# Loading five per-layer vectors as one row and spreading them with a product of ones

## The chip, the core and the metric

The kernel runs on one core of a Trainium2 chip. A core has five engines with queues of their own: TensorE (PE; its weight loads are listed as PEld), VectorE (DVE), ScalarE (ACT), GpSimd (POOL) and SyncE (SP), and sixteen DMA engines that all queues share. DMAs are issued here from SP, ACT and POOL. The metric is the device time of one execution in microseconds, less is better. The times of before are the median of 3 runs, 846.11 us (844.33 to 847.06).

## The reference

A trunk of two layers over 256 tokens of width 1024. Each layer normalises the stream, projects it once into the inputs of three token mixers (a Mamba-2 scan, sliding-window attention with sinks, forgetting attention), gates each branch, projects it back, merges the branches by sigmoid gates, projects once more and adds the residual.

```python
for layer in range(DEPTH):
    h = rms_norm(x, norm_w[layer])
    proj = jnp.einsum('bsd,de->bse', h, w_in[layer])
    ... = jnp.split(proj, split_at, axis=-1)
    y_a = mamba2_branch(a_xbc, a_z, a_dt, conv_w[layer], conv_b[layer], dt_bias[layer],
                        a_log[layer], d_skip[layer], ssm_norm_w[layer])
    y_b = sliding_window_branch(b_q, b_k, b_v, b_z, sinks[layer], cos, sin)
    y_c = forgetting_attention_branch(c_q, c_k, c_v, c_f, c_z, f_bias[layer])
    ...
```

Five of the parameters are vectors of 16 numbers per layer, one number per head. They enter as follows.

```python
dt = jax.nn.softplus(dt_raw + dt_bias)             # step sizes
a = -jnp.exp(a_log)                                # decay rates
y = y + d_skip[:, :, None] * xh                    # skip factors, one per head of 64 channels
sink = jnp.broadcast_to(sinks, ...)                # one more logit in the softmax
log_f = jax.nn.log_sigmoid(f_logit + f_bias)       # forget gates
```

## The kernel before

**Precision and weights.** Every float32 product of the projections is made of three faster passes: an operand is split into a high and a low part, and high x high, low x high and high x low are accumulated. The weights come in parts of 128 partitions x up to 1024 numbers. Each part is loaded by SP into one of six `raw` buffers (`load_part`, L335), split by ACT into `hi` (L257) and by DVE into `lo` (L258), each with six buffers, and then used by PE (`mm`, L97). A raw buffer is free again when its split is done; a hi and lo buffer when PE has used the part.

**Order.** PE's order is written out: the list `ops` holds the blocks of the projections one after the other, and a small planner (`launch`, `pump`) puts the pieces of the mixers (transposes, attention, scan) between the matmuls, by its own clock of PE time. A DMA or operation under `pin` keeps its place in program order; the other engines' orders are chosen when the program is built.

**The start of the first layer.** The first two blocks, the keys and values of the windowed attention, run on the stream before its normalisation; their results are scaled by the row scales `y.rn`. Then `layer_consts` issues the loads of the layer's constants on POOL's queue, and the query blocks and the block of step sizes (`cols(C_DT, 272)`: 16 step-size logits and 256 queries) follow. After that `normalize` is launched: ACT makes a diagonal of the row scales (L1166), PE multiplies it with ones, DVE scales the stream by the product (L1176), and ACT and DVE split it again into the high and low parts that all later blocks use. This stands beside the first block of the forgetting attention's values (`cv(0, 352)`, two halves of 24 matmuls each).

**The constants.** `layer_consts` loads the convolution's weights, its bias and a norm weight into `vr`, 88 rows, which `layer_vec` transposes on PE and copies into `y.vec`. The four vectors dt_bias, f_bias, sinks and a_log are each loaded to all 128 partitions into `y.hb`. The skip factors go to `y.dsk`, where partitions 0 to 63 hold those of the even heads and 64 to 127 those of the odd heads: two loads to 64 partitions, each taking every second number of the row. `logits` adds the parts of `y.hb` to the step-size and forget logits on DVE (L624, L626); `layer_vec` makes `y.nsink` and `y.nega` from it. In the second layer the loads are issued on ACT's queue, late in the first layer, where the norm weight of the second layer is loaded too. `layer_vec` is called just before the first gate block (`zs(C_ZB, 1)`) in both layers.

Of the kernel before, what the change touches and what calls it, by code (L numbers as in the profile page):

```python
# [13 lines left out]
AF = mybir.ActivationFunctionType  # L14
ALU = mybir.AluOpType

P = 128
S = 256
D = 1024
NK = D // P  # L20
# [24 lines left out]
def hybrid_trunk(  # L45
# [5 lines left out]
    nc = tc.nc  # L51
# [11 lines left out]
    def T(tag, shape, dtype=F32, bufs=None):  # L63
        count[0] += 1
        return sb.tile(shape, dtype, tag=tag, name=f"{tag}_{count[0]}",
                       bufs=bufs if bufs is not None else BUFS.get(tag, 1))
# [11 lines left out]
    act = nc.scalar.activation  # L78
# [172 lines left out]
    def pin(f):  # L251
        return lambda *a, **k: tc.keep_in_program_order(f(*a, **k))  # L252
# [141 lines left out]
    for l in range(L):  # L394
        y = Layer()
# [4 lines left out]
    def layer_consts(y, queue):  # L400
        l = y.l
        pdma = pin(queue.dma_start)
        vr = T("vr", [88, P])
        pdma(vr[0:64, :], conv_w[l].rearrange("j (u p) -> (j u) p", p=P))
        pdma(vr[64:80, :], conv_b[l:l + 1, :].rearrange("o (u p) -> (o u) p", p=P))
        pdma(vr[80:88, :], ssm_norm_w[l:l + 1, :].rearrange("o (u p) -> (o u) p", p=P))
        if l:
            y.nwb = T("nwb", [P, D])
            pdma(y.nwb, norm_w[l:l + 1, :].to_broadcast([P, D]))
            pin(nc.gpsimd.tensor_scalar)(y.nwb, y.nwb, -0.5, None, op0=ALU.mult)  # L410
        y.hb = T("hb", [P, 64], bufs=2)
        for i, v in enumerate((dt_bias, f_bias, sinks, a_log)):
            pdma(y.hb[:, 16 * i:16 * i + 16], v[l:l + 1, :].to_broadcast([P, 16]))
        y.dsk = T("dsk", [P, NK], bufs=2)
        for half in range(2):
            src = d_skip[l:l + 1, :].rearrange("o (j two) -> two o j", two=2)[half]
            pdma(y.dsk[64 * half:64 * half + 64, :], src.to_broadcast([64, NK]))
        y.vr = vr

    def layer_vec(y):  # L420
        p = pmx()
        transpose(p[:, 0:88], y.vr, ident[:88, :88])
        y.vec = T("vec", [P, 88], bufs=2)
        act(y.vec[:, 0:80], p[:, 0:80], AF.Copy, scale=0.5)
        act(y.vec[:, 80:88], p[:, 80:88], AF.Copy, scale=-0.5)
        y.nsink = T("nsink", [P, 16], bufs=2)
        pin(ts)(y.nsink, y.hb[:, 32:48], -1.0, None, op0=ALU.mult)
        y.nega = T("nega", [P, 16], bufs=2)
        pin(act)(y.nega, y.hb[:, 48:64], AF.Exp)
        pin(ts)(y.nega, y.nega, -1.0, None, op0=ALU.mult)  # L430


    def chan(y, w, c):
# [71 lines left out]
    def u_bq(y, c0, t):  # L505

        def f(w):
            p = tok(y.hTh, y.hTl, w, t, turn=w.n == 512)
            if w.n == 272:
                logits(y, t, 0, p[:, 0:16])  # L510
                p = p[:, 16:272]
            for i in range(w.n // 256):
                if t == 0:
                    y.qT[c0 + i] = T("qt", [P, 2, S])
                with tc.high_priority():
                    a, b = rope(y, p[:, i, :] if w.n == 512 else p, t)
                    gtt(a, a, b, op=ALU.add)
                launch(1, rest(c0 + i, a.rearrange("p h d -> p (h d)")), D_Q if y.rn is None else 2.2 * D_Q)
            pump()

        def rest(c, q):
            qT = y.qT[c]
            pt = pmx()
            for j in range(2):
                transpose(pt[:, j * P:(j + 1) * P], q[:, j * P:(j + 1) * P], ident)
            act(qT[:, :, t * P:(t + 1) * P], pt[:, 0:256].rearrange("p (h s) -> p h s", h=2), AF.Copy)
            if t == 1:
                launch(1, swa_quad(y, c, qT), D_QK)
            yield 0.0
        return f  # L530
# [527 lines left out]
    def op(i, *fs):  # L1058
        for f in fs:
            ops.append((i, f))  # L1060

    for y in layers:
        l = y.l
        w = w_in[l]
        y.rn = None
        y.gate, y.qT, y.ckT, y.sz, y.yh, y.yl, y.sq, y.h, y.ss, y.var, y.zdone, y.cqdone = {}, {}, {}, {}, {}, {}, [], {}, {}, {}, set(), {}
        y.u = y.cv = None

        def cols(c0, n=256):
            return sub([(0, w[:, c0:c0 + n])], n)  # L1070

        def cv(c, n):
            op(cols(C_CV + c, n), u_cv(y, c, 0), u_cv(y, c, 1))

        def z1(c0, br, b):
            op(cols(c0 + 256 * b), u_z(y, br, 2 * b, 0), u_z(y, br, 2 * b + 1, P))

        def zs(c0, br):
            for b in range(4):
                z1(c0, br, b)  # L1080

        def gates_proj(br):
            def g(b):
                c = 512 * b
                op(cols(C_G + D * br + c, 512), u_gate(y, br, c, 0), u_gate(y, br, c, 1))

            def p(b):
                c = 512 * b
                if b == 0 and br != 0 and (br, l) != (1, 0):
                    op(None, lambda y=y: split_late(y, br))  # L1090
                i = sub([(0, w_proj[l, br, :, c:c + 512])], 512)
                if b == 0 and br == 0:
                    op(i, u_proj2(y, br))
                else:
                    op(i, u_proj(y, br, c, 0), u_proj(y, br, c, 1))
            seq = [(g, 0), (p, 0), (g, 1), (p, 1)]
            if br == 0:
                seq = [(lambda b: z1(C_ZA, 0, b), b) for b in range(4)] + seq
            return [lambda f=f, b=b: f(b) for f, b in seq]

        if l == 0:
            k, v = cols(C_BK), cols(C_BV)
            op(k, u_bkv(y, 0, 0, {16: lambda: second_rows(0), 20: lambda: second_rows(1)}, lambda: first_end()))
            op(k, u_bkv(y, 0, 1, {}))
            op(v, u_bkv(y, 256, 0), u_bkv(y, 256, 1))
            op(None, lambda: layer_consts(y0, nc.gpsimd))
            for c, n in ((1, 512), (3, 256)):
                op(cols(C_BQ + 256 * c, n), u_bq(y, c, 0), u_bq(y, c, 1))
            op(cols(C_DT, 272), u_bq(y, 0, 0), u_bq(y, 0, 1))
            op(None, lambda: launch(9, normalize(y0), 0.0))  # L1110
            cv(0, 352)
            op(None, lambda: normalized(y0))
        else:
            kv, q3 = cols(C_BK, 512), cols(C_BQ + 768)
            op(None, lambda: drain(5))
            op(kv, u_bkv(y, 0, 0))
            op(q3, u_bq(y, 3, 0))
            op(None, lambda: drain(6))
            op(kv, u_bkv(y, 0, 1))
            op(q3, u_bq(y, 3, 1))  # L1120
            op(cols(C_DT, 272), u_bq(y, 0, 0), u_bq(y, 0, 1))
            op(cols(C_BQ + 256, 512), u_bq(y, 1, 0), u_bq(y, 1, 1))
        op(None, lambda y=y: layer_vec(y))
        zs(C_ZB, 1)
        heavy = [(C_B + 256 * b, 8 + 2 * b) for b in range(4)] + [(C_XS + 256 * b, 2 * b) for b in range(4)]
        gp = gates_proj(1)

        if l == 0:
            lights = {1: [lambda: cv(696, 344)], 3: [lambda: cv(352, 344)], 5: [gp.pop(0)], 6: [lambda: op(None, lambda y=y: split_late(y, 1))], 7: [gp.pop(0)]}
        else:  # L1130
            lights = {0: [lambda: cv(696, 344)], 2: [lambda: cv(0, 352)], 3: [lambda: cv(352, 344)],
                      4: [gp.pop(0)], 6: [gp.pop(0)]}
        for i, (c0, u) in enumerate(heavy):
            op(cols(c0), u_conv(y, u, 0), u_conv(y, u + 1, P))
            for light in lights.get(i, ()):
                light()
        for f in gp:
            f()

        for b, zb in enumerate(((), (0,), (1,), (2, 3))):  # L1140
            op(cols(C_CK + 256 * b), u_ck(y, 2 * b, 0), u_ck(y, 2 * b + 1, P))
            op(cols(C_CQ + 256 * b), u_cq(y, 2 * b, 0), u_cq(y, 2 * b + 1, P))
            for z in zb:
                z1(C_ZC, 2, z)
        for f in gates_proj(0):
            f()
        op(None, load_final if l + 1 == L else lambda: layer_consts(layers[1], nc.scalar))
        for f in gates_proj(2):
            f()
        o = [sub([(0, w_out[l, :, c:c + n])], n) for c, n in ((0, 256), (256, 512), (768, 256))]  # L1150
        pieces_out[l] = o[0]
        op(o[0], u_out2(y, 0))
        for t in range(2):
            for i, c in ((1, 256), (2, 768)):
                op(o[i], u_out(y, c, t, i))
# [163 lines left out]
```

## Time and profile before

| | before |
|---|---|
| median of 3 runs | 846.11 us (844.33 to 847.06) |
| profiled execution, time | 846.84 us |
| profiled execution, span from the first to the last instruction | 844.9 us |
| mean granted clock of TensorE | 0.996 |
| PE busy, matmuls | 830.3 us (98%), 6063 |
| DVE busy | 649.7 us (77%) |
| ACT busy | 509.4 us (60%) |
| POOL busy | 105.4 us (12%) |
| moved by DMA | 157.91 MB, mean 187 GB/s |

In the rows of the profile, `out<-in` names the tiles that an instruction writes and reads, L97 is a line of the kernel, and `[3.06 <-ACT L L1166]` says that the engine stood for 3.06 us before the instruction and that line 1166 on ACT ended the wait. A row of the windows gives, for a stretch of the span, its length and the busy time of PE, PEld, DVE, ACT and POOL with their instructions in brackets; then the granted clock, the mean busy share of the DMA engines and GB/s. A DMA row ends with the time from issue to landing. POOL prepares its own DMAs, so they show as rows of POOL; those of SP and ACT stand under SPq and ACTq.

### The profile page before, as it was taken

What the parts mean: (1) busy time and instruction counts of PE and PEld (TensorE: products, weight loads), DVE (VectorE), ACT (ScalarE), POOL (GpSimd) and SP (SyncE); (2) the same over time, 40 slices, a digit from 0 to 9 for tenths busy, and PEclk for the clock granted to TensorE, in tenths of its full rate; (3) what the DMA queues carried; (4) which work ended last, traced back from release to release, by engine and by line L of the source; (5) the groups of instructions that cost most, each with busy time, mean ns of one, the idle gap of its engine ahead of it and who ended that gap; (6) DMA issues with size and microseconds to landing.
All of it is one profiled execution on the core that took longest, in us unless ns stands there. A gap on an engine that the chain in (4) does not pass through costs nothing. (4 is left out here: it accounts for less than half of the span.)

```text
span 844.9 us, 16259 instructions
## 1 busy us (share of the span) xinstructions
PE 830.3 (98%) x6063; PEld 767.9 (91%) x6063; DVE 649.7 (77%) x1425; ACT 509.4 (60%) x1020; POOL 105.4 (12%) x137
## 2 busy tenths in 40 slices
PE   8989999999999999999999999999999999999996
PEld 7989999988999998888989999999899999988896
DVE  6877898998776669656677889889978567785665
ACT  7367777755666667435455676876557667654442
POOL 3810000100140010210013000100003110121000
PEclk9999999999999999999999999999999999999999
DMA  9876456657565545748567535766765554576632
GB/s 305 175 184 184 118 176 206 228 177 233 157 191 177 179 149 178 237 144 297 196 206 221 159 112 161 231 204 203 224 188 176 175 176 150 163 236 212 212 100 74
DMA packets 124495, 157.91 MB, mean 187 GB/s; under 512 B 7321, under 2 KB 91473, under 8 KB 124417
## 3 DMA queue, kind: packets, MB, share of 16 engines
q1 hardware_dynamic: 108816, 140.53, 53.1%
q10 hardware_dynamic: 15312, 16.28, 6.1%
q0 software_dynamic: 288, 0.08, 1.1%
q8 instruction: 47, 0.77, 0.4%
q14 instruction: 32, 0.25, 0.1%
HBM read 154.70 MB, written 2.16 MB: 186 GB/s over the span
## 5 line engine op out<-in xcount | busy, mean ns | idle before, releaser
L258 DVE TENSOR_TENSOR lo<-raw,hi 128x1024 fp32r<-128x1024 f32 (+3 forms) x262 | 309.1, 1194 | 98.1 <-ACT hi L257 86.4
L97 PE MATMUL mm<-hi,L 128*128 128x512 f32 (+4 forms) x1424 | 378.2, 353 | 1.0 <-ACT L L1216 0.5
L257 ACT ACTIVATE hi<-raw 128x1024 fp32r<-128x1024 f32 (+3 forms) x262 | 263.6, 1022 | 97.3 <-PE mm L97 78.7
L97 PE MATMUL mm<-L,hi 128*128 128x256 f32 x1792 | 318.2, 278 | 0.0
L97 PEld LDWEIGHTS mm<-L,hi 128*128 128x128 f32 x1792 | 277.8, 192 | 7.4 <-issue 3.9
L97 PEld LDWEIGHTS mm<-hi,L 128*128 128x128 f32 x1424 | 252.1, 190 | 27.6 <-issue 2.1
L97 PE MATMUL mm<-lo,L 128*128 128x512 f32 (+4 forms) x712 | 247.7, 349 | 0.0
L97 PE MATMUL mm<-L,lo 128*128 128x256 f32 x896 | 246.4, 275 | 0.0
L97 PEld LDWEIGHTS mm<-L,lo 128*128 128x128 f32 x896 | 171.9, 192 | 0.1
L97 PEld LDWEIGHTS mm<-lo,L 128*128 128x128 f32 x712 | 134.8, 190 | 12.4
L872 POOL TENSOR_SCALAR_AFFINE_SELECT bias<-bias 128x128 f32<-128x128 f32 x64 | 36.4, 604 | 413.3 <-DMA bias<-cumd 286.5
L565 ACT ACTIVATE pp<-pp,nm 128x128 f32<-128x128 f32 (+1 forms) x128 | 56.6, 443 | 14.2 <-DVE nm L559 11.8
L694 DVE SCALAR_TENSOR_TENSOR L<-L,vec,L 128x255 f32<-128x255 f32 (+2 forms) x96 | 46.0, 479 | 2.2 <-ACT L L691 1.2
L697 ACT ACTIVATE L<-L 128x256 f32<-128x256 f32 x32 | 13.3, 417 | 42.0 <-DVE L L694 42.0
L896 ACT ACTIVATE L<-L 128x512 f32<-128x512 f32 x24 | 15.1, 630 | 32.6 <-DVE L L895 32.4
L97 PE MATMUL mx<-L,L 128*64 128x128 f32 (+1 forms) x384 | 34.5, 314 | 0.0
L577 DVE TENSOR_SCALAR pp<-pp,rsum 128x128 f32<-128x128 f32 (+1 forms) x128 | 32.1, 314 | 0.3
L778 ACT ACTIVATE L<-mm 128x256 f32<-128x256 f32 x48 | 18.1, 378 | 20.9 <-PE mm L97 20.9
L97 PEld LDWEIGHTS mx<-L,L 128*64 128x64 f32 x384 | 22.9, 136 | 8.3 <-issue 0.9
L594 ACT ACTIVATE L<-mx 128x512 f32<-128x512 f32 x48 | 26.8, 596 | 1.2 <-PE mx L101 1.0
L101 PE MATMUL mx<-ident,pp 128*128 128x128 f32 x192 | 26.3, 273 | 0.0
L565 ACT ACTIVATION_READ_ACCUMULATOR pp<-pp,nm 128x1 f32 x128 | 23.9, 187 | 0.0
(185 smaller groups left out, 718.9 us busy)
## 6 DMA issues: line engine op xcount, KB each, us to landing
raw<-in_w_in_dram SPq DMA_DIRECT2D x179, 512.0 KB, 4.5
raw<-in_w_proj_dram SPq DMA_DIRECT2D x48, 512.0 KB, 5.1
raw<-in_w_out_dram SPq DMA_DIRECT2D x16, 512.0 KB, 5.1
raw<-in_w_in_dram SPq DMA_DIRECT2D x16, 344.0 KB, 3.3
L<-cumd ACTq DMA_DIRECT2D x8, 512.0 KB, 4.9
bias<-cumd ACTq DMA_DIRECT2D x16, 256.0 KB, 3.6
L<-in_gate_bias_dram ACTq DMA_DIRECT2D x12, 256.0 KB, 4.7
raw<-in_w_in_dram SPq DMA_DIRECT2D x8, 352.0 KB, 3.5
```

What stands on the lines that cost most here:

```text
L97: nc.tensor.matmul(o, a, b, **kw)
L101: nc.tensor.transpose(o, a, i)
L257: keep(act)(hi, src, AF.Copy)
L258: keep(tt)(lo, src, hi.bitcast(F32), op=ALU.subtract)
L565: act(pp[:, i, sl], pp[:, i, sl], AF.Exp, scale=-1.0, bias=nm[:, e:e + 1], accum_out=sums[:, e:e + 1])
L577: ts(pp[:, i, sl], pp[:, i, sl], rs[:, 2 * i + b:2 * i + b + 1], 0.5, op0=ALU.mult, op1=ALU.mult)
L594: act(pT, pt, AF.Copy)
L694: stt(a[:, s:S], x_[:, 0:S - s], y.vec[:, 16 * j + u:16 * j + u + 1], a[:, s:S], op0=ALU.mult, op1=ALU.add)
L697: act(th, a, AF.Tanh)
L778: act(halves(th), p, AF.Tanh, scale=0.5)
L872: nc.gpsimd.affine_select(out=bias[:, i, dst], in_=bias[:, i, src], compare_op=ALU.is_ge, fill=NEG, base=0, pattern=[[-1, P]], channel_mul ...
L896: act(g, g, AF.Tanh, scale=0.5)
```

## The change

The five vectors are loaded into one row `y.hr` of one partition (five loads of 16 numbers). `layer_vec` puts the row on all partitions by a product with a row of ones on PE, into the same PSUM bank as the transpose of `vr`, and ACT copies the result into `y.hb`, now 80 columns wide. The skip factors are arranged from it by two copies on POOL, and `y.nsink` and `y.nega` are made on POOL instead of DVE. Since `y.hb` now comes from `layer_vec`, its call moves ahead of the block of step sizes in both layers.

```diff
-        y.hb = T("hb", [P, 64], bufs=2)
-        for i, v in enumerate((dt_bias, f_bias, sinks, a_log)):
-            pdma(y.hb[:, 16 * i:16 * i + 16], v[l:l + 1, :].to_broadcast([P, 16]))
-        y.dsk = T("dsk", [P, NK], bufs=2)
-        for half in range(2):
-            src = d_skip[l:l + 1, :].rearrange("o (j two) -> two o j", two=2)[half]
-            pdma(y.dsk[64 * half:64 * half + 64, :], src.to_broadcast([64, NK]))
+
+        y.hr = T("hr", [1, 80])
+        for i, v in enumerate((dt_bias, f_bias, sinks, a_log, d_skip)):
+            pdma(y.hr[:, 16 * i:16 * i + 16], v[l:l + 1, :])
         y.vr = vr

     def layer_vec(y):
         p = pmx()
         transpose(p[:, 0:88], y.vr, ident[:88, :88])
         y.vec = T("vec", [P, 88], bufs=2)
-        act(y.vec[:, 0:80], p[:, 0:80], AF.Copy, scale=0.5)
-        act(y.vec[:, 80:88], p[:, 80:88], AF.Copy, scale=-0.5)
-        y.nsink = T("nsink", [P, 16], bufs=2)
-        pin(ts)(y.nsink, y.hb[:, 32:48], -1.0, None, op0=ALU.mult)
+        mm(p[:, 96:176], ones[0:1, :], y.hr, start=True, stop=True)
+        y.hb = T("hb", [P, 80], bufs=2)
+        pin(act)(y.hb, p[:, 96:176], AF.Copy)
+        pin(act)(y.vec[:, 0:80], p[:, 0:80], AF.Copy, scale=0.5)
+        pin(act)(y.vec[:, 80:88], p[:, 80:88], AF.Copy, scale=-0.5)
         y.nega = T("nega", [P, 16], bufs=2)
         pin(act)(y.nega, y.hb[:, 48:64], AF.Exp)
-        pin(ts)(y.nega, y.nega, -1.0, None, op0=ALU.mult)
+        gts = nc.gpsimd.tensor_scalar
+        y.nsink = T("nsink", [P, 16], bufs=2)
+        gts(y.nsink, y.hb[:, 32:48], -1.0, None, op0=ALU.mult)
+        gts(y.nega, y.nega, -1.0, None, op0=ALU.mult)
+        y.dsk = T("dsk", [P, NK], bufs=2)
+        for i in range(2):
+            r = slice(64 * i, 64 * i + 64)
+            nc.gpsimd.tensor_copy(y.dsk[r, :], y.hb[r, 64:80].rearrange("p (j i) -> p i j", i=2)[:, i, :])
...
             for c, n in ((1, 512), (3, 256)):
                 op(cols(C_BQ + 256 * c, n), u_bq(y, c, 0), u_bq(y, c, 1))
+            op(None, lambda y=y: layer_vec(y))
             op(cols(C_DT, 272), u_bq(y, 0, 0), u_bq(y, 0, 1))
...
             op(kv, u_bkv(y, 0, 1))
             op(q3, u_bq(y, 3, 1))
+            op(None, lambda y=y: layer_vec(y))
             op(cols(C_DT, 272), u_bq(y, 0, 0), u_bq(y, 0, 1))
             op(cols(C_BQ + 256, 512), u_bq(y, 1, 0), u_bq(y, 1, 1))
-        op(None, lambda y=y: layer_vec(y))
         zs(C_ZB, 1)
```

## The prediction

> **What bounds the kernel now.** I read the page first (busy times, queues), then the waits of PE, then the timeline around the one long wait, then the windows and the DMA issues of that stretch.
>
> ```profile
> PE 830.3 (98%) x6063; PEld 767.9 (91%) x6063; DVE 649.7 (77%) x1425; ACT 509.4 (60%) x1020; POOL 105.4 (12%) x137
> q0 software_dynamic: 288, 0.08, 1.1%
> ```
>
> PE is busy for 830.3 of 844.9 us, so an edit is worth what it does to PE's queue: work added, waits removed, clock. The second row is the queue of the DMAs that POOL issues: 0.08 MB cost 1.1% of sixteen engines' span, which is 0.011 x 844.9 = 9.3 us on every engine. All POOL DMAs are the loads of the first layer's constants, in one stretch.
>
> ```profile
> PE mx L97 <- ACT L L1166: 3.1, 1, 3.1
> PE mx L101 <- POOL ident masks.py:199: 1.5, 1, 1.5
> ```
>
> The longest wait of PE is one of 3.1 us; the next is at the start. It stands here in the timeline:
>
> ```profile
> 47.85 0.46 PE L97 MATMUL mm<-hi,L 128*128 128x352 f32 x2
> ...
> 48.30 0.46 PE L97 MATMUL mm<-hi,L 128*128 128x352 f32 x2
> ...
> 48.75 0.38 PE L101 MATMUL mx<-ident,L 128*128 128x128 f32 x2
> 50.79 1.06 ACT L257 ACTIVATE hi<-raw 128x1024 fp32r<-128x1024 f32 x1 [5.67 <-DMA raw<-in_w_in_dram]
> 51.75 0.68 ACT L1166 ACTIVATE L<-ident,rs 128x128 f32<-128x128 f32 x2
> ...
> 52.19 1.09 PE L97 MATMUL mx<-L,ones 128*128 128x128 f32 x4 [3.06 <-ACT L L1166]
> ```
>
> Read it backwards. PE waits for the diagonal of row scales (`normalize`); ACT made it only at 51.75, because a weight split stood ahead of it in ACT's order, and that split waited 5.67 us for its weights. The weights were late because the DMA engines were full and moved nothing:
>
> ```profile
> 34.00:38.00 4.00, 4.00 (x35) 4.00 (x35) 1.83 (x5) 0.79 (x1) 3.98 (x7) 1.00 0.95 171
> 38.00:42.00 4.00, 4.00 (x35) 4.00 (x34) 3.31 (x7) 1.09 (x3) 1.59 (x2) 1.00 1.07 38
> 42.00:48.00 6.00, 6.00 (x47) 5.99 (x46) 3.79 (x9) 2.22 (x4) 2.31 (x2) 1.00 0.67 5
> 48.00:52.00 4.00, 1.13 (x9) 0.88 (x7) 0.12 (x1) 1.21 (x2) 0.00 (x0) 1.00 0.91 310
> 52.00:56.00 4.00, 3.81 (x15) 3.81 (x16) 3.88 (x7) 3.49 (x9) 0.00 (x0) 0.57 1.10 351
> ```
>
> The last three columns are granted clock, DMA share and GB/s. From 38 to 48 us the engines show shares of 1.07 and 0.67 at 38 and 5 GB/s. In the last row the clock is 0.57: after its wait PE runs at about half speed for some 4 us.
>
> ```profile
> 31.90 0.37 SPq L335 DMA_DIRECT2D raw<-in_w_in_dram  x1
> 40.83 4.50 SPq L335 DMA_DIRECT2D raw<-in_w_in_dram  x1
> DMA to landing us min/median/max: 3.0/4.4/17.6
> vr<-in_conv_w_dram POOLq DMA_DIRECT2D x1, 32.0 KB, 2.2
> vr<-in_ssm_norm_w_dram POOLq DMA_DIRECT2D x1, 4.0 KB, 3.5
> hb<-in_sinks_dram POOLq DMA_DIRECT2D x1, 8.0 KB, 7.6
> dsk<-in_d_skip_dram POOLq DMA_DIRECT2D x2, 2.0 KB, 14.1
> ```
>
> The weight load that ACT waited for is the one issued at 31.90 (six raw buffers, so its turn comes with the split six parts earlier). The third row is for weight loads between 20 and 70 us: median 4.4, longest 17.6. One issue took 4.50 us instead of 0.37. The two d_skip loads, 2 KB each, take 14.1 us: they are 512 single numbers each, written with a stride over 64 partitions. They are what runs while everything else stands.
>
> **The change part by part.**
>
> (a) The scattered skip-factor loads and the four 128-partition loads go; five loads of one row of 64 bytes come. With them goes the blockage of 38 to 48 us. The load of 31.90 then lands at 31.90 + 4.4 = 36.3, an estimate from the median. What is late next?
>
> ```profile
> 44.05 1.06 ACT L257 ACTIVATE hi<-raw 128x1024 fp32r<-128x1024 f32 x1 [0.34 <-PE mm L97]
> ```
>
> This split comes just ahead of the blocked one and waits for PE to free a buffer, so ACT is at the blocked one at 44.05 + 1.06 = 45.1. In the changed program's order two query copies then stand ahead of the diagonal: 45.1 + 1.06 + about 0.65 + 0.68 = 47.5. PE asks for it at 48.75 plus two transposes, 49.0. So the 3.06 us go whole, and with them the slow clock: (1 - 0.57) x 4.0 = 1.7 us. Together **-4.8 us**.
>
> The Trainium skill (TensorE: Matmul & The Clock Gate, Part 1) says the clock falls to half after an idle window of about 3.4 us and recovers after as long a busy one. The row of 52 to 56 us agrees in kind, but the wait was only 3.06 us, so I count 3 us as the limit, not 3.4.
>
> (b) Behind it the normalised stream must be ready when PE has done the second half of the value block.
>
> ```profile
> 53.31 1.88 DVE L1176 TENSOR_TENSOR L<-L,mx 128x512 f32<-128x512 f32 x3
> 56.44 2.00 DVE L258 TENSOR_TENSOR L<-L,L 128x512 fp32r<-128x512 f32 x3
> ```
>
> PE's product began at 52.19 and DVE's last piece ended at 58.44, 6.25 us later, of which about 0.4 was PE's slow clock. At full clock the half block is eight groups of 0.45 us (47.85 to 48.30) = 3.6, plus product and transposes 0.65: PE is back for the new stream after 4.25 us. It needs the first half of the channels then (their low parts end with the first of the last three pieces, 56.44 + 0.67 = 57.1, so 4.5 after the product at full clock) and the rest 1.35 later. That is a new wait of 0.2; if PE had to have the whole stream it would be 1.6. I take **+0.2**, by the pieces' own tiles, and keep 0 to 1.6.
>
> (c) PE gets one more product per layer (80 columns from one row); the 88-column transpose only moves.
>
> ```profile
> 58.24 0.24 PE L101 MATMUL mx<-ident,vr 88*128 88x88 f32 x1
> 61.12 1.58 PE L97 MATMUL mx<-L,qt 64*128 64x128 f32 x16
> L97 PE MATMUL mx<-L,ones 128*128 128x128 f32 x36 | 6.0, 291 | 3.1 <-ACT L L1166 3.1
> ```
>
> Sixteen records are eight products (two records each) in 1.58 us: 0.2 each. Not overlapped it would be 2 x 0.291 = 0.6; fewer columns could make it 0.1. I take 0.2, the pipelined row, since PE streams on: **+0.4** for both layers, ends 0.2 and 1.2.
>
> (d) The vectors are now needed by PE itself, ahead of the block with the step sizes.
>
> ```profile
> 32.86 0.54 POOL L252 DMA_DIRECT2D hb<-in_a_log_dram  x1
> 33.40 1.40 POOL L252 DMA_DIRECT2D dsk<-in_d_skip_dram  x2
> 38.27 0.41 PE L97 MATMUL mm<-hi,L 128*128 128x272 f32 x2
> ```
>
> Five loads at 0.54 take the slots from 31.20 on, so the last is issued at 33.4, where d_skip is issued now. PE reaches the product at 38.27: 4.9 us later. The small direct loads of this queue land in 2.2 to 3.5, so at 35.6 to 36.9, 1.4 us before PE. Queued behind the product on PE is everything, so a late row is paid in full; at hb's 7.6 it lands at 41.0 and costs 2.7. I take **0**, by the vr rows: like those, the new loads are direct and tiny, while hb and dsk queue up behind their own small pieces.
>
> (e) ACT gets the eviction of the vectors, and it, the two scaled copies and the exponential move ahead of the query copies; DVE loses two small products per layer; POOL gets four.
>
> ```profile
> 59.00 0.23 ACT L424 ACTIVATE vec<-mx 128x80 f32<-128x80 f32 x1
> 2.45 0.10 POOL L187 MEMSET mhalf<- 128x8 f32 x1
> L224 POOL TENSOR_TENSOR sm<-sm,mhalf 128x1 f32<-128x1 f32 x4 | 3.2, 801 | 124.6 <-DVE sm L252 124.6
> 41.70 0.66 ACT L526 ACTIVATE qt<-mx 128x256 f32<-128x256 f32 x2 [2.56 <-PE mx L101]
> 41.49 0.23 DVE L626 SCALAR_TENSOR_TENSOR u<-mm,rs,hb 128x16 f32<-128x16 f32 x1 [0.69 <-PE mm L97]
> ```
>
> Four ACT operations of 0.23 fall into ACT's pause of 2.56 before 41.70: nothing. Four on POOL cost 0.1 to 0.8 each, 0.4 to 3.2 in all; behind them wait three rotary sums, whose transposes come 8 us and more later on PE; the step-size logits (the last row) wait for ACT's eviction, ready by about 39.4, and are due at 41.5. So 0, and at the most 0.5 if POOL is at its slow end.
>
> (f) The second layer's loads are on ACT's queue.
>
> ```profile
> 363.61 1.34 ACTq L252 DMA_DIRECT2D dsk<-in_d_skip_dram  x2
> 365.05 3.15 ACT L257 ACTIVATE hi<-raw 128x1024 fp32r<-128x1024 f32 x3 [5.93 <-DMA hb<-in_dt_bias_dram]
> 350.00:380.00 30.00, 30.00 (x140) 26.27 (x140) 16.28 (x18) 11.14 (x13) 5.34 (x3) 1.00 0.55 176
> ```
>
> ACT stands 5.93 us for them, but PE is busy 30.00 of 30.00 us there. About 1 us less of it gains nothing; the vectors are used only in the second layer, long after.
>
> Sum: -4.8 + 0.2 + 0.4 = -4.2. The profiled execution took 846.84 (span 844.9), so 842.6; it lies 0.73 above the median of 846.11, so **841.9** against the median. PE is the bound from 58 us to the end, so what is gained stays gained.
>
> **The rivals.** About 0.3%, 2.5 us, is what a measurement of this kernel tells from no change.
>
> *The row lands late, like hb* (7.6 us): PE waits 2.7 us at 38.3, short of the 3.06 that cost the clock. 841.9 + 2.7 = 844.6, within 0.3%. For it: same queue, DMA share 0.95 then. Against: hb's own pieces made that share. The Trainium skill (SBUF — State Buffer, the "DVE blocks DMA" trap) says POOL's descriptors starve while DVE holds the shared port; by it this rival would come about. That POOL's issues keep to 0.54 speaks against it here, but its landings of 7.6 leave it open.
>
> *The row lands like dsk* (slower): 64 bytes as sixteen single numbers, 14.1 us from 33.4, at 47.5. PE waits 9.2 and loses the clock, 1.7 more: 841.9 + 10.9 = 852.8. It decides from a wait of 5.0 us, a landing 9.9 us after the last issue (4.2 + 2.5 = 5.0 + 1.7). Against: 80 numbers instead of 1,024. The Trainium skill (DMA: Bandwidth & Descriptors, How many engines) says such a row is split so that it spreads over the engines; no run here shows it yet.
>
> *The blockage is not dsk's alone, or PE meets the next late split*: half the wait stays, the clock is kept or not. Gains of 0 to 2.5: 843.6 to 846.1, within 0.3%. For it: six raw loads in flight. Against: weight loads land in 4.4 elsewhere.
>
> **How the numbers follow.** Forecast 0.72, late row 0.10, blockage stays 0.10, row like dsk 0.08. Run scatter (844.33 to 847.06) puts a twentieth of the forecast inside 0.3%. Faster 0.68, same 0.24, slower 0.08. The range goes from 841.9 less the scatter, 840.0, to beyond the late row and the whole-stream wait, 845.3.
>
> **What would show it.** Right: no PE wait on the diagonal; clock 1.0 through 48 to 60 us; over 100 GB/s between 38 and 44; q0 under 0.4%; the product of (d) without a wait over 0.5. Wrong: a PE wait on hr at 38 us, or ACT's splits still waiting on raw there; then (d) or (a) is the failed step.

## The result and the profile after

The changed kernel takes 841.9 us (median of 10 executions, 840.82 to 842.7), the kernel before beside it 846.77 us (10 executions, 844.33 to 850.45): a ratio of 0.9941, interval 0.9926 to 0.9956. The profiled execution of after took 840.82 us, its span is 839.1 us, the mean granted clock 0.999.

From the page of after, PE's row of busy times and POOL's DMA queue (packets, MB, share of sixteen engines' span):

```profile
PE 830.2 (99%) x6067; PEld 768.3 (92%) x6067; DVE 650.0 (77%) x1421; ACT 510.9 (61%) x1022; POOL 108.1 (13%) x144
q0 software_dynamic: 256, 0.05, 0.0%
```

PE is busy for as long as before (830.3), four matmul records more included; the span is 5.8 us shorter. So the gain is waiting, not work. POOL's queue went from 1.1% to 0.0%. The waits of PE in after, all that the view lists:

```profile
PE mx L101 <- POOL ident masks.py:199: 1.5, 1, 1.5
PE mm L97 <- ACT L L257: 0.3, 1, 0.3
PE mm L97 <- DVE L L258: 0.2, 1, 0.2
```

The wait on the diagonal is gone. The windows of after (length and busy times of PE, PEld, DVE, ACT, POOL; granted clock, DMA share, GB/s), first over the stretch of the prediction, then in the second layer:

```profile
34.00:38.00 4.00, 4.00 (x36) 3.87 (x34) 3.18 (x5) 0.89 (x2) 3.55 (x5) 1.00 0.84 266
38.00:42.00 4.00, 4.00 (x32) 3.92 (x32) 2.27 (x7) 1.22 (x6) 2.29 (x5) 1.00 0.76 222
42.00:48.00 6.00, 6.00 (x47) 6.00 (x46) 4.66 (x10) 4.48 (x9) 2.38 (x2) 1.00 0.46 147
...
52.00:56.00 4.00, 4.00 (x35) 4.00 (x33) 4.00 (x7) 4.00 (x8) 0.00 (x0) 1.00 0.08 27
...
368.00:372.00 4.00, 4.00 (x20) 3.52 (x19) 1.43 (x2) 0.40 (x1) 0.00 (x0) 1.00 0.93 280
384.00:388.00 4.00, 4.00 (x20) 3.52 (x19) 2.97 (x3) 3.29 (x4) 0.00 (x0) 1.00 0.15 45
```

Where 38 and 5 GB/s were moved, 222 and 147 are now, and the clock stays at 1.00. The last two rows stand for a second difference, which the prediction did not see. The same stretch of the kernel before, with the wait of PE that lies in it:

```profile
364.00:368.00 4.00, 4.00 (x21) 3.49 (x20) 1.86 (x3) 2.87 (x3) 2.79 (x1) 1.00 0.35 107
368.00:372.00 4.00, 4.00 (x20) 3.52 (x19) 4.00 (x4) 3.71 (x5) 0.00 (x0) 1.00 0.05 0
372.00:376.00 4.00, 4.00 (x21) 3.49 (x20) 2.24 (x3) 0.70 (x2) 0.00 (x0) 1.00 0.04 2
...
384.00:388.00 4.00, 3.12 (x15) 2.40 (x13) 4.00 (x5) 2.20 (x3) 0.00 (x0) 1.00 1.06 361
```

```profile
PE mx L101 <- DVE L L945: 1.2, 1, 1.2
```

In the second layer too, where the loads were on ACT's queue, the scattered skip factors stopped the weights: 0 and 2 GB/s for 8 us. PE had buffered parts and ran on; but from 380 on ACT and DVE caught up with the late weights at 361 GB/s, and 11 us after the blockage PE stood 1.2 us for DVE. In after the wait is gone.

Two stretches of PE's timeline in after, the moved transpose with the new product, and the product of the row scales up to the first blocks on the normalised stream:

```profile
37.83 0.24 PE L101 MATMUL mx<-ident,vr 88*128 88x88 f32 x1
38.00 0.44 PE L97 MATMUL mx<-hr,ones 1*128 1x80 f32 x2
38.37 0.52 PE L97 MATMUL mm<-hi,L 128*128 128x272 f32 x2
...
49.16 0.61 PE L97 MATMUL mx<-L,ones 128*128 128x128 f32 x4
...
53.41 0.27 PE L97 MATMUL mm<-L,hi 128*128 128x256 f32 x1
...
53.63 0.40 PE L97 MATMUL mm<-L,hi 128*128 128x256 f32 x2
```

The last row is at 58.58 in the kernel before. Of the 4.95 us between them, 0.44 lie ahead of the change and are not its work (PE is at this point of its order at 37.83 instead of 38.27), so the stretch gained 4.51 net, in which a product of some 0.5 is paid. With the 1.2 us of the second layer and another such product there, 0.44 + 4.51 + 1.2 - 0.5 = 5.65 of the 5.8 us are found.

### The profile page after: what moved, and what is told of

Read it like the earlier page. It is cut to its first block, busy times and chain, and to the rows that moved or that the text cites. A ratio compares the mean times of both kernels' runs of the same rounds, so it can differ in the third digit from the quotient of the medians.

```text
span 839.1 us, 16279 instructions
## 1 busy us (share of the span) xinstructions
PE 830.2 (99%) x6067; PEld 768.3 (92%) x6067; DVE 650.0 (77%) x1421; ACT 510.9 (61%) x1022; POOL 108.1 (13%) x144
## 4 chain that ended last, share of the span: by engine, by line
PE 99%; DVE 0%; ACT 0%; issue 0%; POOLq 0%; POOL 0%
PE mm L97 84%; PE mx L97 10%; PE mx L101 5%; DVE L L258 0%; DVE L L1218 0%; POOLq L1321 0%; ACT L L1031 0%; DVE L L1226 0%; ACT L L257 0%; DVE L L1006 0%; DVE L L1010 0%; POOL ident masks.py:199 0%; DVE sm L226 0%; POOL tri L168 0%; DVE sm L252 0%
## 5 line engine op out<-in xcount | busy, mean ns | idle before, releaser
L900 DVE TENSOR_TENSOR L<-mm,L 128x512 f32<-128x512 f32 x24 | 16.4, 684 | 9.7 <-PE mm L97 9.7
```

The source lines that it names most:

```text
L900: tt(halves(g), p, halves(y.gb), op=ALU.add)
```

## The experiments

Every time below is a median; each ratio is to the kernel before, timed beside it on the same chip.

**What in the two loads costs so much: the count of pieces.** The two loads stay where they are, to the same partitions with the same bytes, but read eight neighbouring numbers instead of every second one. The heads get each other's skip factors by it, so only the time is of use.

```diff
-            src = d_skip[l:l + 1, :].rearrange("o (j two) -> two o j", two=2)[half]
+            src = d_skip[l:l + 1, NK * half:NK * half + NK]
```

> The kernel before with the two skip-factor loads unchanged in place, queue, partitions and bytes, but each reads eight neighbouring numbers instead of every second one, so a partition's part is one piece of 32 bytes: 128 pieces instead of 1,024. The skip factors of the heads come out in the wrong order. Theory (the count of single numbers is the cost): the blockage goes in both layers, no window under 100 GB/s between 34 and 48 us or 364 and 376, landings of 5 to 8 us like hb's, no wait on the diagonal; 840.5 to 841.5, like the version with one more 128-partition load. Rival (loads to many partitions are the cost, whatever their pieces): blockage as before, 845 to 847.

Measured: 840.05 us, ratio 0.9937 (0.9916 to 0.9957). From its page the queue, and its windows:

```profile
q0 software_dynamic: 288, 0.08, 0.3%
```

```profile
38.00:42.00 4.00, 4.00 (x35) 4.00 (x34) 3.11 (x7) 0.88 (x2) 1.59 (x2) 1.00 0.96 189
42.00:48.00 6.00, 6.00 (x47) 5.99 (x47) 4.59 (x10) 4.62 (x9) 2.31 (x2) 1.00 0.83 264
...
368.00:372.00 4.00, 4.00 (x21) 3.49 (x20) 2.37 (x4) 0.63 (x1) 0.00 (x0) 1.00 0.95 305
```

The queue's packets and bytes are those of before (288, 0.08; so its packets do not count the pieces), its time is 0.3% instead of 1.1%, and no window is blocked in either layer. ACT's queue, which has the loads of the second layer, does show the pieces, in the kernel before and in this one:

```profile
q10 hardware_dynamic: 15312, 16.28, 6.1%
q10 hardware_dynamic: 14416, 16.28, 5.9%
```

These are 896 packets fewer, 1,024 - 128. So neither the 64 partitions nor the queue is the price, but 1,024 pieces of four bytes in place of 128 of 32. For POOL's queue, 0.8% of 844.9 us is 6.8 us on each engine for (1,024 - 128) / 16 = 56 more pieces: about 0.12 us apiece, an estimate from these rows. The Trainium skill (DMA: Bandwidth & Descriptors, Rules for kernel authors) says that a last dimension that is not contiguous becomes one descriptor per element, and tells the author to rearrange it; this run agrees.

**The skip factors alone.** The kernel before with d_skip as a fifth load to 128 partitions, arranged by two POOL copies at the end of `layer_vec`. No product, no row, nothing moved.

```diff
-        y.hb = T("hb", [P, 64], bufs=2)
-        for i, v in enumerate((dt_bias, f_bias, sinks, a_log)):
+        y.hb = T("hb", [P, 80], bufs=2)
+        for i, v in enumerate((dt_bias, f_bias, sinks, a_log, d_skip)):
...
+            pin(nc.gpsimd.tensor_copy)(y.dsk[r, :], y.hb[r, 64:80].rearrange("p (j i) -> p i j", i=2)[:, i, :])
```

> The kernel before, with one edit: d_skip is loaded to all partitions like the other four vectors (a fifth 128-partition load of 8 KB) and arranged by two copies on POOL at the end of layer_vec. No product, nothing moved. Theory (the scattered skip loads block the DMA engines): the PE wait on the diagonal goes, GB/s between 38 and 48 us over 100, about 841.5 us, ratio 0.994. Rival A (the 128-partition loads block): five of them stay, so the wait stays, 846.8, ratio 1.000. Rival B (the move of layer_vec and of the query transposes, or the POOL arithmetic, made the difference): 846.8, ratio 1.000.

Measured: 840.54 us, ratio 0.9937 (0.9917 to 0.9957). Its windows:

```profile
38.00:42.00 4.00, 4.00 (x35) 4.00 (x34) 3.31 (x7) 1.07 (x2) 1.61 (x2) 1.00 0.96 186
42.00:48.00 6.00, 6.00 (x47) 5.99 (x46) 4.59 (x10) 4.43 (x9) 2.50 (x3) 1.00 0.78 252
```

The whole gain comes with the skip factors alone. The four 128-partition loads, still there, do no harm here.

**Half of the scatter.** One of the two scattered loads stays, the other half comes from such a fifth load.

```diff
-        for half in range(2):
-            src = d_skip[l:l + 1, :].rearrange("o (j two) -> two o j", two=2)[half]
-            pdma(y.dsk[64 * half:64 * half + 64, :], src.to_broadcast([64, NK]))
+        src = d_skip[l:l + 1, :].rearrange("o (j two) -> two o j", two=2)[0]
+        pdma(y.dsk[0:64, :], src.to_broadcast([64, NK]))
```

> The kernel before, with one of the two scattered skip loads (partitions 0 to 63); the other half is arranged on POOL from a fifth 128-partition load. Theory: half of the blockage, about 4 us less of it; the weight load of 31.9 us lands near 46, ACT makes the diagonal at 47 to 49, PE waits 0 to 1 us for it and keeps its clock: 841.8 to 843.5, ratio 0.994 to 0.996, so most of the gain for half of the removal. A loss in proportion would be 844.3, ratio 0.997. Rivals A and B: 846.8, ratio 1.000.

Measured: 840.75 us, ratio 0.9935 (0.9911 to 0.9959). Its windows:

```profile
34.00:38.00 4.00, 4.00 (x36) 4.00 (x36) 4.00 (x11) 0.52 (x2) 2.25 (x3) 1.00 1.20 7
38.00:42.00 4.00, 4.00 (x35) 4.00 (x34) 2.91 (x7) 1.18 (x2) 2.71 (x3) 1.00 0.44 154
```

The weights stand again, at 7 GB/s, but for some 5 us instead of 8, and it costs nothing that these times show (840.54 us without the scatter): PE has parts for that time. The price of a blockage has a threshold; it is not proportional.

**The row for four vectors, the scatter kept.** The changed kernel, but the skip factors come by the two scattered loads.

```diff
-        y.hr = T("hr", [1, 80])
-        for i, v in enumerate((dt_bias, f_bias, sinks, a_log, d_skip)):
+        y.hr = T("hr", [1, 64])
+        for i, v in enumerate((dt_bias, f_bias, sinks, a_log)):
             pdma(y.hr[:, 16 * i:16 * i + 16], v[l:l + 1, :])
+        y.dsk = T("dsk", [P, NK], bufs=2)
+        for half in range(2):
+            src = d_skip[l:l + 1, :].rearrange("o (j two) -> two o j", two=2)[half]
+            pdma(y.dsk[64 * half:64 * half + 64, :], src.to_broadcast([64, NK]))
```

> The changed kernel, with one edit: the skip factors are loaded by the two scattered loads as before; the other four vectors come as a row of 64 and by the product, layer_vec stays moved. Theory: the wait of about 3 us on the diagonal and the half clock behind it are back, 847 us, ratio 1.000 to 1.001. Rival A: 842.0 to 842.5, ratio 0.994 to 0.995. Rival B: 842.0, ratio 0.994.

Measured: 842.93 us, ratio 0.9973 (0.9951 to 0.9994). Its windows and its longest wait of PE:

```profile
38.00:42.00 4.00, 4.00 (x33) 3.91 (x32) 2.55 (x7) 1.21 (x6) 1.77 (x3) 1.00 1.00 1
...
48.00:52.00 4.00, 3.92 (x29) 3.66 (x27) 3.06 (x5) 3.42 (x9) 0.02 (x1) 1.00 1.09 351
...
368.00:372.00 4.00, 4.00 (x20) 3.50 (x19) 4.00 (x6) 2.40 (x3) 0.00 (x0) 1.00 0.04 0
...
384.00:388.00 4.00, 2.72 (x12) 2.34 (x13) 3.12 (x5) 1.79 (x3) 0.00 (x0) 0.83 1.00 348
388.00:392.00 4.00, 4.00 (x16) 3.31 (x15) 2.25 (x2) 2.06 (x3) 0.00 (x0) 0.74 0.46 160
```

```profile
PE mx L101 <- DVE L L950: 2.4, 1, 2.4
```

The time is 4 us under the 847 that was expected, and 3.1 under the kernel before (846.0 beside it): much of the gain comes although the scatter stays. The blockage is back in the first layer (1 GB/s), and yet PE hardly waits there (3.92 of 4.00 busy): it is over some 3 us sooner (the split waits until 47.50 instead of 50.79), which is just in time. The pieces of the four 128-partition loads, which no longer stand ahead of the scatter, would account for that. It is not shown by itself: this version moves `layer_vec` too, and the version below with only the second layer arranged, whose first layer is written as before, reached the same split at 48.57 in its profiled execution. The loss is in the second layer, 2.4 us of wait, and about 1.7 of clock ((1 - 0.83) x 4 + (1 - 0.74) x 4). So in the first layer of the kernel before it seems to be the scatter and the broadcast pieces together that cost; the broadcast pieces alone (second experiment) and the scatter alone (here) left PE no long wait there.

**Each layer for itself.** Arranged skip factors as in the second experiment, in one layer; the other layer keeps the scatter.

```diff
+        for i, v in enumerate((dt_bias, f_bias, sinks, a_log) + ((d_skip,) if l == 0 else ())):
```

> The kernel before, with the skip factors arranged on POOL in the first layer only; the second layer keeps its two scattered loads on ACT's queue. Theory as revised (two blockages, one in each layer): no wait on the diagonal, but still no weight loads for about 8 to 12 us after 360 us, and a PE wait of 0.5 to 2.4 us for the merge near 384 us; 841.5 to 843, ratio 0.995 to 0.997, its runs spread over 2 us or more. Theory as predicted (the second layer's loads cost nothing): the time of the kernel with both layers arranged, 840.5, ratio 0.9935, with its narrow spread of about 1 us.

> The other half: skip factors arranged on POOL in the second layer only; the first layer keeps its scattered loads. Theory as revised: the wait on the diagonal of about 3 us and the half clock stay, the wait near 384 us goes: 844 to 845.5, ratio 0.997 to 0.999. Theory as predicted: 846.0 to 846.8, ratio 1.000.

Measured: 842.29 us with the first layer arranged (ratio 0.998, 0.9959 to 1.0001), 842.9 us with the second (0.9979, 0.9955 to 1.0003); the version with both, timed beside them, 840.52 us (0.9944, 0.9921 to 0.9966). By these intervals neither is told from the kernel before, nor the two shares from each other, and the second came out under the 844 to 845.5 that was expected. But the waits of PE show a share in each layer. First layer arranged, then second layer arranged:

```profile
PE mx L101 <- DVE L L951: 1.1, 1, 1.1
```

```profile
PE mx L97 <- ACT L L1172: 1.0, 1, 1.0
```

Each layer's scatter has its own wait of about 1 us here. The second row is the wait of 3.1 us of the kernel before, in an execution where it came out at 1.0 and the clock stayed at 1.00, which fits the lower time. Its length seems to vary from execution to execution: in 85 timed executions of the kernel before, 37 had a mean clock of 0.996 or less and took 845.31 to 850.03 us (median 847.58), 48 had 0.997 or more and took 841.56 to 847.97 (median 844.10). That the clock falls or not as this wait comes out longer or shorter fits these times; no profile of these executions shows it.

**Another place.** The kernel before, with the scattered loads of the first layer issued after `layer_vec`, at 47.6 and 48.3 us.

```diff
+        if l == 0:
+            op(None, lambda y=y: skip_scatter(y, nc.gpsimd))
         zs(C_ZB, 1)
```

> The kernel before, with the first layer's two scattered skip loads issued on POOL after layer_vec instead of before the query blocks, some 25 us later, at about 55 to 58 us; all else as before. Theory: the same 7 to 10 us without weight loads come there, and since six raw parts are 16 us of PE's work in 256-column blocks, PE does not feel them: 842, ratio 0.994. If the blockage costs wherever it stands, a PE wait of 2 to 4 us comes there and the time is 845 to 847. Rivals A and B: 846.8, ratio 1.000.

Measured: 842.22 us, ratio 0.9954 (0.9932 to 0.9976). Its window:

```profile
52.00:56.00 4.00, 4.00 (x36) 3.88 (x34) 4.00 (x6) 4.00 (x10) 0.00 (x0) 1.00 0.75 0
```

The time is that of the version with the first layer arranged (842.29 us): the blockage costs nothing here. Nothing is moved for these 4 us and PE is busy throughout: here the loads have a natural pause, as the row of after at the same place shows (27 GB/s). So the same blockage costs only what the buffered parts can't cover.

**Another queue.** The kernel before, with the scattered loads of the first layer on ACT's queue, as in the second.

```diff
-            pdma(y.dsk[64 * half:64 * half + 64, :], src.to_broadcast([64, NK]))
+            pin(nc.scalar.dma_start)(y.dsk[64 * half:64 * half + 64, :], src.to_broadcast([64, NK]))
```

> The kernel before with only the two scattered skip-factor loads of the first layer issued from ACT's queue instead of POOL's (in the second layer they are there already). Theory (the 1,024 single numbers themselves hold the sixteen engines, whoever issues them): a stretch of 8 us or more with under 50 GB/s between 30 and 50 us, as in the second layer of the kernel before, where they went from ACT's queue and windows showed 0 to 2 GB/s; time within 2 us of the kernel before, 844 to 848. Rival (it is the queue of POOL's DMAs, whose descriptors are prepared in software): no window under 100 GB/s in the first layer, no wait on the diagonal, 842 to 843.

Measured: 845.02 us, ratio 0.999 (0.9968 to 1.0011). Its windows, and two of its waits of PE:

```profile
24.00:28.00 4.00, 4.00 (x20) 3.53 (x19) 4.00 (x6) 0.39 (x1) 4.00 (x2) 1.00 0.16 31
28.00:30.00 2.00, 2.00 (x11) 1.74 (x10) 2.00 (x5) 1.38 (x2) 2.00 (x3) 1.00 0.05 1
```

```profile
PE mm L97 <- DVE L L469: 1.9, 1, 1.9
PE mx L101 <- DVE L L945: 1.6, 1, 1.6
```

ACT reached its issue at 21.4 us instead of 33, so the stretch expected from 30 on lies from 24 on, with under 50 GB/s for 6 us instead of 8 or more; the cost moved with it, to a wait of 1.9 us at 40 us. It is not POOL's queue alone that blocks. But the expected way, that the numbers hold the sixteen engines, is not shown for ACT's queue: the engines' shares are 0.16 and 0.05 here, and 0.05 and 0.04 in the second layer of the kernel before, where POOL's queue showed 1.07 and 0.67. What holds the weights up there stays open.

**The row on PE's path.** The changed kernel itself, timed beside the one-layer versions.

> The changed kernel once more, on the same chip as the next one: 841.9, ratio 0.994. Theory: it pays for two products, the transpose beside them and their weight loads some 0.5 us per layer, which the next one doesn't.

Measured: 842.34 us (841.24 to 844.98), ratio 0.9964 (0.9948 to 0.998). In its profiled execution PE waits for the row:

```profile
PE mx L97 <- DMA hr<-in_d_skip_dram: 1.1, 1, 1.1
```

Then with the transpose and the product ahead of the 256-column query block of the first layer, one block sooner.

```diff
             for c, n in ((1, 512), (3, 256)):
+                if c == 3:
+                    op(None, lambda y=y: layer_vec(y))
                 op(cols(C_BQ + 256 * c, n), u_bq(y, c, 0), u_bq(y, c, 1))
-            op(None, lambda y=y: layer_vec(y))
```

> The changed kernel with one step moved: in the first layer the transpose of the constants and the product of the row with ones come ahead of the 256-column query block instead of behind it, so PE asks for the row some 6 us sooner, at about 32 us instead of 38. Theory (the row is a chain of its own, landed at about 37.6 whoever waits for it, because its loads are issued on POOL up to 33 us and take 4 to 5 us to land): PE waits 5 to 6 us there, longer than the 3.06 us that already cost the clock in the kernel before, so a half clock of some 1.7 us follows; 841.9 + 5.5 + 1.7 = 849. Rival A (the wait is given back, because weight parts pile up and the split engines get ahead while PE stands): 842 to 845. Rival B (the loads land sooner when PE is not streaming): a wait of 3 us, 845.

Measured: 848.98 us (842.66 to 850.32), ratio 1.0039 (1.0016 to 1.0062). PE's timeline and the windows behind it:

```profile
34.94 0.27 PE L101 MATMUL mx<-ident,vr 88*128 88x88 f32 x1 [1.68 <-DMA vr<-in_ssm_norm_w_dram]
...
38.55 0.68 PE L97 MATMUL mx<-hr,ones 1*128 1x80 f32 x2 [3.35 <-DMA hr<-in_d_skip_dram]
```

```profile
38.00:42.00 4.00, 3.45 (x15) 3.33 (x16) 0.00 (x0) 0.53 (x4) 1.53 (x5) 0.50 0.29 96
42.00:48.00 6.00, 6.00 (x42) 6.00 (x42) 2.04 (x5) 1.25 (x2) 0.74 (x1) 0.76 0.00 0
```

The row lands at its own time, at about 38.4 us, 4.6 after its last issue (4.7 and 6.0 in the two profiles of the changed kernel), whoever waits for it. PE's waits are 1.68 + 3.35 = 5.0 us, the clock costs about 0.5 x 3.45 + 0.24 x 6 = 3.2 more. Nine of the ten executions took 847.70 to 850.32 us; one took 842.66 at a mean clock of 0.998, and no profile shows why. So a late row is paid in full, and the row of the change lies one block away from being slower than before. It is the rival's mechanism, made to happen.

**What is best.** The second experiment's kernel again, beside the changed kernel.

> The kernel before with a fifth 128-partition load for d_skip and two copies on POOL, no product, nothing moved, beside the changed kernel: 840.6, ratio 0.9925 to 0.994, 0.5 to 1.4 us under the changed kernel. If the product and the move are worth something beyond the scatter, it is slower than the changed kernel.

Measured: without the row and the products 840.52 us (840.54 the first time), and 842.34 for the changed kernel beside it. This version beats both kernels, the changed one by 1.8 us. Two products of 0.5 us, and a wait for the row of 0 or 1.1 us, make 1.0 to 2.1.

## Why the prediction was right, and where it was not

The sign, the mechanism and the median came as said. That 841.9 us met 841.9 exactly is partly luck: the kernel before came out at 846.77 over ten executions instead of 846.11, and two errors have opposite signs, (c) too cheap by 0.6 us and (f) without its 1.2. Between the two profiled executions the span fell by 5.8 us, 1.6 more than the sum of 4.2.

(a) Right. The chain of scattered numbers, standing weights, late split, late diagonal and lost clock is shown by the loads with neighbouring numbers, which change the pieces alone. ACT made the diagonal at 46.68 + 0.69 = 47.4 us (47.5 said). Too simple was "They are what runs while everything else stands", of the two d_skip loads: with the scatter alone, and the broadcast pieces gone, PE hardly waited in the first layer. The stride, too, is in what these loads read; the eight numbers that they write to a partition stand side by side. The rival "the blockage is not dsk's alone" had that part right, though not its outcome, as after has neither.

(b) Too dear by its 0.2. PE was back for the stream at 53.41, 4.25 us after the product as worked out, and did not wait: the stream was ready.

(c) Mis-sized. Transpose and product take 0.54 us of PE (37.83 to 38.37), not the 0.2 of the pipelined row; the transpose before cost 0.03 (58.24 to 58.27). In the second layer it is the same 0.54 (439.70 to 440.24). That is 0.5 in each layer, 1.0 in all instead of 0.4, near the upper end of 1.2. The row chosen was one where sixteen alike follow each other; a single product between two unlike neighbours doesn't overlap so.

(d) Right in the profiled execution, by less than thought. The DMA issues of after, first and last of the row:

```profile
hr<-in_dt_bias_dram POOLq DMA_DIRECT2D x1, 0.1 KB, 3.9
...
hr<-in_d_skip_dram POOLq DMA_DIRECT2D x1, 0.1 KB, 4.7
```

They land in 3.9 to 4.9 us, not in the 2.2 to 3.5 of the vr rows, so the last is there at about 37.6 and the margin to PE's 38.0 is 0.4 us, not 1.4. In the other profiled execution PE waited 1.1 us: the rival of the late row, at 1.1 of its 2.7 us. The Trainium skill (SBUF — State Buffer, the "DVE blocks DMA" trap) would have POOL's descriptors late; the issues kept to 0.48 to 0.50 us, and no run here tells whether the landings of 4.7 come from that. The row like dsk did not come: 4.9 us at the most in after and 6.0 in the other profiled execution, not 14.1.

(e) Right: no wait of PE comes from ACT's or POOL's new operations, though the two copies on POOL take 1.17 us.

(f) Wrong. "Gains nothing" was argued from PE's 30.00 of 30.00 busy us between 350 and 380. The price lies behind that window: 1.2 us of wait at 387 in the kernel before, 2.4 and the clock in the version that keeps the scatter, 1.1 with only the first layer arranged. With it falls "PE is the bound from 58 us to the end". A blockage must be followed to where the buffers run dry, not only through its own duration.

## What to carry to other kernels

A load of a few kilobytes can hold up some hundred times its bytes when it is cut into single numbers (here 4 KB against about 1.5 MB, an estimate from 8 us at the mean of 187 GB/s): count the pieces of each DMA, load contiguous runs, and arrange them on chip on an engine that has time. After a stretch with no GB/s look at the next 20 us of the busiest engine, since prefetched buffers hide the cause from the effect. And a tiny load that the bounding engine itself waits for is dearer than a larger one that it does not need: the 128-partition loads landed after up to 8.5 us and cost nothing, the row lands after 5 to 6 and sometimes does.

## What the runs showed of the hardware

1,024 numbers of four bytes, from POOL's queue or from ACT's, leave 0 to 5 GB/s to all others for some 8 us (40 to 48 and 368 to 376 us in the kernel before); in the first layer ACT's queue left under 50 GB/s for 6 us. From POOL's queue that is about 0.12 us of an engine for each, an estimate as above; from ACT's the engines show shares of only 0.04 to 0.16 meanwhile. Half as many, from POOL's queue, leave 7 GB/s for about 5 us.

The granted clock fell to 0.50 in three of these profiles and stayed there for 3.4 us or twice as long, read in windows of 1 us and less: from 52.4 to 55.8 us after a wait of 3.06 us (the kernel before), from 386.7 to 390.0 after one of 2.4 (the scatter kept), and from 38.0 to 44.9 with waits of 1.68 and 3.35 just before (the product earlier). So 0.57, 0.83 and 0.74 in the rows are means over 4 us of the same drop, which cost 1.7 us where it lasted 3.4. In the second case PE had been back for 1.4 us when the clock fell. It stayed at 1.00 after waits of 1.9, 1.6, 1.2, 1.1 and 1.0. The Trainium skill (TensorE: Matmul & The Clock Gate, Part 1) gives an idle window of about 3.4 us, free-running; waits of 2.4 and 3.06 us were enough here. If a length alone decides, it lies between 1.9 and 2.4 us by these few waits, but they do not show that it does.
